# Two squares summed on TensorE, and a rule by which the planner lets an engine wait

## The chip, the cores and the metric

The kernel runs on one core of a Trainium2 chip. A core has TensorE (PE, matmuls into PSUM), VectorE (DVE), ScalarE (ACT), GpSimd (POOL) and SyncE (SP), which issues most of the DMAs. The metric is the time of one execution on the device in microseconds (us), taken as the median of several runs. The profile is of one more execution; its rows give times from the start of its span.

## What is computed

Two layers work on 512 latent tokens of width 1024 with a prefix of 256 context tokens. Each layer normalises and modulates the tokens, makes one wide projection, runs three kinds of attention over groups of its columns, gates the result and projects it back:

```python
def layer(x, cx, ...):
    mod = c_silu @ ada_w + ada_b                      # mod_c likewise, for the context
    shift, scale, gate = split(mod, 3)
    hx = rmsnorm(x, norm_w) * (1 + scale) + shift     # hc likewise
    px, pc = split_cols(hx @ w_in), split_cols(hc @ w_in)
    ya = global_gqa(...)            # all latent and context keys, rotary, normalised q and k
    yb = neighbourhood_attn(...)    # a clamped 2-D window, learned bias
    yc = window_gqa(...)            # +-128 tokens, a sink logit
    ux = concat(ya, yb, yc) * silu(px[9])
    x = x + gate * (ux @ w_out)
```

`rmsnorm(x, w)` is `x * rsqrt(mean(x*x) + 1e-6) * w`. After the second layer the latent tokens are normalised once more and returned. The context is carried only as far as the second layer needs it.

## The kernel before

**Tiling.** Activations are held transposed: width on the 128 partitions, in 8 blocks (`KT = 8`), tokens along the free dimension. The latent set is 128x512 a block, the context set 128x256. All products are fp32 made of two parts: a tensor is split into a rounded high part and a low part (names ending in h and l: `wh`/`wl`, `hL` for latent and `hC` for context activations), and PE adds three matmuls for each product. `split` does that for weights: `ws` arrives by DMA, ACT rounds it to `wh` (L245), DVE or POOL subtracts for `wl` (L248). In the attention, `pth` and `ptl` are the two parts of a transposed P, `P` the weights of the softmax; P goes to memory and comes back gathered as `R` (tiles R5 and R2), which PE transposes (L1049). `negm` (L1218) is the row maximum that the next stage waits for, and `OT` (L1069) gathers the attention's output from the bank `Obig`.

**The first norm.** `load_x(0)` issues eight DMAs for the latent blocks, `load_x(1)` eight for the context. `norm_x(s)` calls `add_sq` for each of the eight blocks of set `s`: ACT squares the block (L342), DVE adds the square to the first one (L346), and at the eighth PE multiplies the sum with a column of ones (L350), once for each 128 tokens (four times for the latent set, twice for the context), into the bank `Obig`. `rstd_rows` scales that (L357), POOL raises it to the power -1/2 (L359), PE spreads the result over the partitions (L367), and ACT copies it as `rb` (L390). `make_h` multiplies each block by it and by the modulation (L397) and splits it into `hL` or `hC` (L398, L400), with which the first projections start (L419). Beside it runs the modulation: `ada` multiplies silu(c) with weights that stream in (L213), ACT copies (L217, `adasb`), PE transposes (L221) and DVE finishes (L224 to L230, into tiles `mod`).

**The change of layers.** While the last attention of a layer runs, `reload` brings its gated results back (`uf`) and splits them (L481) into `qt`, `kt`, `hL`, `hC` and others; these are names of buffers that are used again, and here they hold the input of the output projection. `head` begins the output projection of the first blocks (`out_mm`, L508) in the `pj` and `Sbig` banks, and `block` finishes each: it loads the old stream `xr` by DMA (L551), DVE adds it times the gate to the bank (L561, `xn`), and `add_sq` starts the next norm's sum. DVE also computes part of the second layer's modulation itself, as dot products (L154): the gate from tiles `dots` of 128x512 (their DMAs L171 and L175, `junk512` their unused elementwise result), and the shift from rows: `row` (L682) holds silu(c) spread over the partitions and `dw` (L689) the weights, two dots of 128x1024 for each of eight `dw`. The tiles `row`, `dw` and `kept` (output weights that stay, split at L248 too) share one set of buffers in a pool that opens when buffers of the layer before are released, among them `hC` (L481) and `u` (L1377, L1379).

**What sets the order.** No order is written by hand. `arrange` takes all instructions as `Step`s with a modelled cost (`busy`, and for DMAs `move`), builds their dependences in a `Graph`, and calls `run(rank)`: a list schedule over five engines, in modelled time. Each engine takes, of the instructions that are ready by now (`now[e]`), the one of the best rank; those that get ready later are in `later[e]`. A rank is minus the time that still lies behind the instruction on its longest path, in ns, so a smaller rank is more urgent. `back` finds these times from a finished schedule, and the loop goes six turns, each with the ranks of the turn before. The schedule with the earliest modelled end gives each engine's stream, which is then fixed by added dependences:

```python
    for _ in range(CFG["turns"]):
        start, end, busy, streams = graph.run(rank)
        if best is None or max(end) < best[0]:
            best = max(end), streams
        at = graph.back(start, end, busy)
        rank = [(-t, k) for k, t in enumerate(at)]
```

So on the chip each engine works through a fixed list and waits, in order, for the next instruction's inputs.

Of the kernel before, what the change touches and what calls it, by code (L numbers as in the profile page):

```python
# [21 lines left out]
KT = 8  # L22
# [43 lines left out]
def body(tc, xT, small, bcast, rpb, adaw, adat, wt, wf, wo, trigA, trigQ, trigC, mskB, mskC, outT):  # L66
    nc = tc.nc
# [16 lines left out]
    ones = const.tile([128, 2], F32)  # L84
# [26 lines left out]
    Obig = ps.tile([128, 512], F32)  # L111
# [158 lines left out]
    def en(kind):  # L270

        turn[kind] = turn.get(kind, -1) + 1
        return nc.vector if EN[kind][turn[kind] % len(EN[kind])] == "D" else nc.gpsimd
# [62 lines left out]
            with tc.high_priority(offset=CFG["hp"]):  # L336
                done(p[:, 0:512].rearrange("p (t c) -> p t c", t=2), t2)

    def add_sq(sums, x, kt, n, pool, bank=psO):

        sq = pool.tile([128, NT], F32, name="sq", bufs=3)
        nc.scalar.activation(sq[:, 0:n], x, AF.Square)  # L342
        if kt == 0:
            sums.append(sq)
            return
        en("sq").tensor_add(sums[0][:, 0:n], sums[0][:, 0:n], sq[:, 0:n])  # L346
        if kt == KT - 1:
            pss = bank()
            for t in range(n // 128):
                nc.tensor.matmul(pss[:, 2 * t:2 * t + 2], sums[0][:, t * 128:(t + 1) * 128], ones,  # L350
                                 start=(t == 0), stop=True, skip_group_check=True)
            sums.append(pss)

    def rstd_rows(pss, n, pool, out):
        k = n // 128
# [17 lines left out]
    with tc.tile_pool(name="p0", bufs=1, reuse_waits="tile") as p0:  # L373
        xs = {}
# [9 lines left out]
        def norm_x(s):  # L384
            n = SETS[s][1] - SETS[s][0]
            sums = []
            for kt in range(KT):
                add_sq(sums, xs[s, kt], kt, n, p0, lambda: Obig[:, s * 8:])
            r = p0.tile([128, n], F32, name=f"rb{s}")
            nc.scalar.activation(r, rstd_rows(sums[1], n, p0, Sbig[:, s * 512:s * 512 + n])[:, 0:n], AF.Copy)  # L390
            rb[s] = r
# [137 lines left out]
    for l in range(2):  # L529
# [3 lines left out]
        with tc.tile_pool(name=f"p2_{l}", bufs=1, reuse_waits="tile") as p2:  # L533
# [139 lines left out]
            xs, sums = ({}, {}), ([], [])  # L673
# [67 lines left out]
            n = 0  # L741
# [853 lines left out]
BANKS = ("pj", "T", "Sbig", "Obig")  # L1595
TO_PE, TO_OTHER, TO_LAND = 400.0, 150.0, 700.0
SLOW = 21000.0
ISSUE = dict(tB=580.0, R5=520.0, R2=520.0, wr=680.0)
WAIT = {"PE": 53.0, "POOL": 78.0, "ACT": 36.0, "DVE": 36.0, "SP": 30.0}
BEHIND = {"ACT": 112.0, "DVE": 85.0, "POOL": 45.0}  # L1600
# [93 lines left out]
class Graph:  # L1694
# [76 lines left out]
    def run(self, rank):  # L1771

        steps, n = self.steps, len(self.steps)
        left = [len(b) for b in self.before]
        ready = [0.0] * n
        start, end, spent = [0.0] * n, [0.0] * n, [0.0] * n
        later = {e: [] for e in ENGINES.values()}
# [25 lines left out]
        while done < n:  # L1803
# [13 lines left out]
                    heapq.heappush(now[e], ((-1e18, 0), min(same)[1]))  # L1817
            r, k = heapq.heappop(now[e])
            s = steps[k]
            need, wait = t, None  # L1820
            for name in self.opens[k]:
                tag = self.tag[name]
# [246 lines left out]
```

## Time and profile before

| | us |
|---|---|
| median of 3 runs | 1146.3 |
| lowest, highest | 1142.51, 1149.14 |
| the profiled execution, device time | 1148.5 |
| its span | 1146.7 |
| PE busy (7352 records) | 1106.9 (97%) |
| DVE busy | 778.3 (68%) |
| ACT busy | 675.8 (59%) |
| POOL busy | 401.1 (35%) |

The span runs from the first to the last instruction; the device time of the same execution is 1.8 us longer. A row of the timeline gives start and length in us, engine, line, operation, output <- inputs (buffer numbers left out), the shapes, how many records are taken together, and in brackets the idle time ahead with what ended it. A matmul of fp32 that is not split shows as two records. `SPq` is the sequencer of SP while it issues DMAs. A row of a list of waits gives the waiting instruction, what released it, and the total, the number and the longest of these waits. Matmuls overlap their successors, so a record's length is more than its distance to the next.

### The profile page before, as it was taken

To read this page: it belongs to the slowest core of one execution; us is meant where nothing else is said; L and a number is where in the kernel's file an instruction comes from. 1 tells how busy PE (TensorE), PEld (TensorE's weight loads), DVE (VectorE), ACT (ScalarE), POOL (GpSimd) and SP (SyncE) were. 2 spreads that over 40 slices of the span, in tenths; PEclk is the share of its full clock that TensorE was granted. 3 is DMA by queue.
4 is the path that set the end of the run, shared out by engine and by line. 5 is a ranking of instruction groups with operands and counts; after the bars stand their busy time and mean duration, and the time that the engine had idled before them with its cause. 6 is when DMAs were issued, how large, how long until landed. Compare 5 with 4: busy or idle time off the path is not lost.

```text
span 1146.7 us, 21341 instructions
## 1 busy us (share of the span) xinstructions
PE 1106.9 (97%) x7352; PEld 974.5 (85%) x7352; DVE 778.3 (68%) x1642; ACT 675.8 (59%) x1454; POOL 401.1 (35%) x352
## 2 busy tenths in 40 slices
PE   5999999999999999999899999999999999999996
PEld 3799989998888888888687989998988888888886
DVE  5767667656657777668879764778565567677753
ACT  5546556465656667768623643555556677778651
POOL 1542102145452364526400021221156656556001
PEclk8999999999999999999999999999999999999998
DMA  9455446445464555456768543555344554557452
GB/s 356 180 154 191 140 135 193 137 152 165 157 204 151 191 174 185 160 186 217 252 227 267 166 148 98 169 182 152 126 144 157 161 180 163 194 177 228 140 175 74
DMA packets 111541, 200.96 MB, mean 175 GB/s; under 512 B 13676, under 2 KB 32456, under 8 KB 111432
## 3 DMA queue, kind: packets, MB, share of 16 engines
q1 hardware_dynamic: 103440, 184.01, 49.3%
q10 hardware_dynamic: 7992, 15.58, 4.1%
q8 instruction: 58, 0.95, 0.4%
q14 instruction: 51, 0.42, 0.1%
HBM read 116.46 MB, written 11.25 MB: 111 GB/s over the span
## 4 chain that ended last, share of the span: by engine, by line
PE 79%; DMA 6%; DVE 5%; ACT 3%; issue 3%; POOL 3%; SPq 1%; ACTq 0%; DVEq 0%; POOLq 0%
PE pj L311 29%; PE Obig L1033 9%; PE Sbig L1033 9%; PE T L1049 6%; PE pj L332 6%; PE pj L508 5%; DMA R<-P 4%; PE T L508 4%; PE Sbig L508 2%; PE Sbig L419 2%; PE T L311 2%; PE pj L419 1%; DVE junk L154 1%; PE Sbig L332 1%; DMA dw<-adat_dram 1%
## 5 line engine op out<-in xcount | busy, mean ns | idle before, releaser
L311 PE MATMUL pj<-hL,wh 128*128 128x512 f32 x880 | 293.1, 399 | 0.7 <-ACT tR L995 0.5
L1029 DVE TENSOR_TENSOR ptl<-T,pth 128x512 fp32r<-128x512 f32 (+1 forms) x264 | 172.5, 670 | 70.4 <-ACT pth L781 68.2
L781 ACT ACTIVATE pth<-T 128x512 fp32r<-128x512 f32 (+1 forms) x264 | 147.3, 580 | 73.3 <-PE T L1049 64.4
L311 PEld LDWEIGHTS pj<-hL,wh 128*128 128x128 f32 x880 | 158.8, 188 | 27.3 <-issue 1.7
L311 PE MATMUL pj<-hL,wl 128*128 128x512 f32 x440 | 174.8, 397 | 0.0
L245 ACT ACTIVATE wh<-ws 128x512 fp32r<-128x512 f32 x192 | 119.9, 629 | 93.1 <-PE pj L311 37.4
L1033 PE MATMUL Sbig<-kt,qt 128*128 128x256 f32 (+1 forms) x864 | 159.4, 305 | 0.9 <-DVE negm L1218 0.8
L248 POOL TENSOR_TENSOR wl<-ws,wh 128x512 fp32r<-128x512 f32 x76 | 100.2, 1320 | 145.1 <-ACT wh L245 126.0
L1033 PEld LDWEIGHTS Sbig<-kt,qt 128*128 128x128 f32 x864 | 127.6, 189 | 11.2 <-DVE negm L1218 1.8
L1049 PEld LDWEIGHTS T<-identr,R 128*128 128x128 f32 x1024 | 106.8, 140 | 27.4 <-DMA R<-P 7.4
L1033 PE MATMUL Obig<-pth,vt 128*128 128x256 f32 (+2 forms) x432 | 125.9, 307 | 2.2 <-DVE OT L1069 1.5
L1033 PE MATMUL Obig<-ptl,vt 128*128 128x256 f32 (+2 forms) x432 | 123.8, 306 | 0.2
L1049 PE MATMUL T<-identr,R 128*128 128x128 f32 x1024 | 114.5, 242 | 8.4 <-DMA R<-P 7.2
L248 DVE TENSOR_TENSOR wl<-ws,wh 128x512 fp32r<-128x512 f32 x116 | 84.9, 738 | 40.2 <-ACT wh L245 30.0
L311 PE MATMUL pj<-hC,wh 128*128 128x256 f32 x512 | 98.8, 284 | 0.0
L311 PEld LDWEIGHTS pj<-hL,wl 128*128 128x128 f32 x440 | 82.7, 188 | 15.0 <-issue 0.9
L1033 PEld LDWEIGHTS Obig<-pth,vt 128*128 128x128 f32 x432 | 81.3, 188 | 10.1 <-DVE OT L1069 2.1
L1033 PEld LDWEIGHTS Obig<-ptl,vt 128*128 128x128 f32 x432 | 81.2, 188 | 6.1 <-DVE negm L1117 0.5
L311 PEld LDWEIGHTS pj<-hC,wh 128*128 128x128 f32 x512 | 82.1, 190 | 2.1 <-DVE rs L881 0.2
L1115 DVE CUSTOM_DVE_ANT_0 P<-Sbig,rs 128x768 f32<-128x768 f32 (+1 forms) x80 | 65.7, 845 | 25.5 <-PE Sbig L1033 17.9
L1118 ACT ACTIVATE P<-P,negm 128x768 f32<-128x768 f32 (+1 forms) x80 | 67.5, 846 | 22.5 <-DVE negm L1117 16.7
L1459 POOL TENSOR_TENSOR bm<-wr,bm 128x192 f32<-128x192 f32 (+1 forms) x48 | 41.6, 893 | 97.3 <-DMA bm<-mskB_dram 64.6
(340 smaller groups left out, 2288.4 us busy)
## 6 DMA issues: line engine op xcount, KB each, us to landing
R<-P SPq DMA_DIRECT2D x216, 256.0 KB
ws<-wf_dram SPq DMA_DIRECT2D x120, 256.0 KB
ada<-adaw_dram SPq DMA_DIRECT2D x32, 512.0 KB
ws<-wo_dram SPq DMA_DIRECT2D x57, 256.0 KB
bm<-mskB_dram SPq DMA_DIRECT2D x16, 576.0 KB
R<-P SPq DMA_DIRECT2D x64, 128.0 KB
ws<-wt_dram SPq DMA_DIRECT2D x24, 256.0 KB
tB<-tA SPq DMA_DIRECT2D x72, 64.0 KB
```

Of the source, the lines that this page charges most:

```text
L245: nc.scalar.activation(hi, src, AF.Copy)
L248: eng.tensor_sub(lo, src, hi.bitcast(F32))
L311: nc.tensor.matmul(p[:, 0:n], a[:, r, :], cols(b[kt], c0, n), start=(i == 0), stop=(i == 23))
L332: nc.tensor.matmul(p[:, t * 256:(t + 1) * 256], tok(a[kt], t2 + t), b[:, r, :], start=(i == 0), stop=(i == 23))
L508: nc.tensor.matmul(p[:, 0:n], a[:, r, :], ucols(ua[b][ft], c0, n), start=(ft == FT_ORDER[0] and i == 0), stop=(ft == FT_ORDER[-1] and i == 2))
L781: nc.scalar.activation(out, src, AF.Copy)
L1029: nc.vector.tensor_sub(lo[:, 0:n], T[:, 0:n], hi[:, 0:n].bitcast(F32))
L1033: return nc.tensor.matmul(*args, **kw)
L1049: return nc.tensor.transpose(out.bitcast(F32R), src, identr)
L1115: nc.vector.tensor_tensor_reduce(out=P, in0=S, in1=r.to_broadcast([128, n]), op0=OP.mult, op1=OP.max, scale=1.0, scalar=-3.0e38, accum_out=m)
L1118: nc.scalar.activation(P, P, AF.Exp, bias=nm, accum_out=unit.stat("sums", i))
L1459: nc.gpsimd.tensor_add(b, src, b)
```

## The change

It has two parts. In `add_sq`, the squares of the last two latent blocks of the first norm (`alone`, blocks 6 and 7) are no longer added on DVE. PE multiplies the sum of blocks 0 to 5 with the ones (four matmuls), then the square of block 6 (four), then that of block 7 (four), all accumulating in the bank: twelve matmuls in place of four, and five adds in place of seven. Added dependences (`after`) keep them behind the first of them. The context set and all other norms take the old path.

In `run`, an engine other than PE looks ahead before it takes an instruction. If one that is more urgent by over 3000 ns (`HOLD`) gets ready before the one at hand would be done (`long`, for a DMA the longer of issue and transfer), the engine takes only an instruction that ends by then (60 ns of grace) or else stays idle until then. The rule acts in the model, when the order is made; on the chip only the order differs.

```diff
--- before.py
+++ after.py
@@ -336,20 +336,29 @@
             with tc.high_priority(offset=CFG["hp"]):
                 done(p[:, 0:512].rearrange("p (t c) -> p t c", t=2), t2)
 
-    def add_sq(sums, x, kt, n, pool, bank=psO):
+    sums_first = []
+
+    def add_sq(sums, x, kt, n, pool, bank=psO, alone=()):
 
         sq = pool.tile([128, NT], F32, name="sq", bufs=3)
         nc.scalar.activation(sq[:, 0:n], x, AF.Square)
         if kt == 0:
             sums.append(sq)
             return
-        en("sq").tensor_add(sums[0][:, 0:n], sums[0][:, 0:n], sq[:, 0:n])
-        if kt == KT - 1:
-            pss = bank()
+        if kt not in alone:
+            en("sq").tensor_add(sums[0][:, 0:n], sums[0][:, 0:n], sq[:, 0:n])
+        if kt == KT - 1 - len(alone):
+            sums.append(bank())
+            sq = sums[0]
+        if len(sums) == 2:
             for t in range(n // 128):
-                nc.tensor.matmul(pss[:, 2 * t:2 * t + 2], sums[0][:, t * 128:(t + 1) * 128], ones,
-                                 start=(t == 0), stop=True, skip_group_check=True)
-            sums.append(pss)
+                m = nc.tensor.matmul(sums[1][:, 2 * t:2 * t + 2], sq[:, t * 128:(t + 1) * 128], ones,
+                                     start=(len(sums) == 2 and t == 0 and kt == KT - 1 - len(alone)), stop=kt == KT - 1,
+                                     skip_group_check=True)
+                if alone and (t or kt > KT - 1 - len(alone)):
+                    after(m, sums_first[0])
+                elif alone:
+                    sums_first[:] = [m.ins.name]
 
     def rstd_rows(pss, n, pool, out):
         k = n // 128
@@ -385,7 +394,7 @@
             n = SETS[s][1] - SETS[s][0]
             sums = []
             for kt in range(KT):
-                add_sq(sums, xs[s, kt], kt, n, p0, lambda: Obig[:, s * 8:])
+                add_sq(sums, xs[s, kt], kt, n, p0, lambda: Obig[:, s * 8:], () if s else (KT - 2, KT - 1))
             r = p0.tile([128, n], F32, name=f"rb{s}")
             nc.scalar.activation(r, rstd_rows(sums[1], n, p0, Sbig[:, s * 512:s * 512 + n])[:, 0:n], AF.Copy)
             rb[s] = r
@@ -1595,6 +1604,7 @@
 BANKS = ("pj", "T", "Sbig", "Obig")
 TO_PE, TO_OTHER, TO_LAND = 400.0, 150.0, 700.0
 SLOW = 21000.0
+HOLD = dict(DVE=3000.0, ACT=3000.0, POOL=3000.0, SP=3000.0)
 ISSUE = dict(tB=580.0, R5=520.0, R2=520.0, wr=680.0)
 WAIT = {"PE": 53.0, "POOL": 78.0, "ACT": 36.0, "DVE": 36.0, "SP": 30.0}
 BEHIND = {"ACT": 112.0, "DVE": 85.0, "POOL": 45.0}
@@ -1817,6 +1827,20 @@
                     heapq.heappush(now[e], ((-1e18, 0), min(same)[1]))
             r, k = heapq.heappop(now[e])
             s = steps[k]
+            if e in HOLD:
+                long = max(s.busy, s.move) if s.dma else s.busy
+                soon = [x for x, y, _ in later[e] if y[0] < r[0] - HOLD[e] and x < t + long]
+                if soon:
+                    x = min(soon)
+                    fit = [z for z in now[e] if t + steps[z[1]].busy <= x + 60]
+                    heapq.heappush(now[e], (r, k))
+                    if not fit:
+                        free[e] = x
+                        continue
+                    r, k = min(fit)
+                    now[e].remove((r, k))
+                    heapq.heapify(now[e])
+                    s = steps[k]
             need, wait = t, None
             for name in self.opens[k]:
                 tag = self.tag[name]
```

Lines from 346 on stand 3 to 9 lines later in the changed kernel, and those behind `HOLD` 10 and more; L508 there is L517, L154 and L213 keep their numbers. Buffers from the first norm on have numbers 6 higher (`pj_6946` becomes `pj_6952`).

**The start, on PE.** The first rows of PE's stream before; `sq_151` is the sum of the squares, `ada` weights of the modulation, `T` a bank, `pj_219` the bank of the first projection:

```order
L350 MATMUL Obig_94<-ones_83,sq_151 128x2 x4
L213 MATMUL T_247<-ada_131,silu_c_95 2x256 x4
L213 MATMUL T_247<-ada_133,silu_c_95 2x256 x4
L367 MATMUL Sbig_93<-ident_72,rstd_179 128x128 x4
L221 MATMUL T_247<-ident_72,adasb_257 128x128 x2
L213 MATMUL T_312<-ada_221,silu_c_95 2x256 x4
L142 MATMUL T_369<-ident_72,silu_c_95 128x128 x4
L213 MATMUL T_312<-ada_223,silu_c_95 2x256 x4
L221 MATMUL T_312<-ident_72,adasb_322 128x128 x2
L350 MATMUL Obig_94<-ones_83,sq_187 128x2 x2
L419 MATMUL pj_219<-hL_243,wh_227 128x512
```

The same in the changed kernel (`sq_172` and `sq_178` are the squares of blocks 6 and 7):

```order
L355 MATMUL Obig_94<-ones_83,sq_151 128x2 x4
L355 MATMUL Obig_94<-ones_83,sq_172 128x2 x4
L355 MATMUL Obig_94<-ones_83,sq_178 128x2 x4
L213 MATMUL T_253<-ada_131,silu_c_95 2x256 x4
L213 MATMUL T_253<-ada_133,silu_c_95 2x256 x4
L376 MATMUL Sbig_93<-ident_72,rstd_185 128x128 x4
L221 MATMUL T_253<-ident_72,adasb_263 128x128 x2
L213 MATMUL T_318<-ada_227,silu_c_95 2x256 x4
L213 MATMUL T_318<-ada_229,silu_c_95 2x256 x4
L142 MATMUL T_375<-ident_72,silu_c_95 128x128 x4
L221 MATMUL T_318<-ident_72,adasb_328 128x128 x2
L142 MATMUL T_454<-ident_72,silu_c_95 128x128 x4
```

The two new groups stand behind the sum, ahead of the modulation's matmuls; behind them the two groups on `ada_227` and `ada_229` now stand together, and a second L142 group has come ahead of the context's sums and the first projection, which follow behind these rows.

**Near the end of the first layer's attention, on PE.** Before, two first matmuls that need `kt_6919` stand ahead of transposes of `R` (`T_7236<-identr` is the last of them); behind these come the other four on it, and only then those of another output block, in `Sbig`:

```order
L1049 MATMUL T_7236<-identr_77,R5_7183 128x128
L1049 MATMUL T_7236<-identr_77,R5_7206 128x128
L508 MATMUL pj_6946<-kt_6919,wh_6942 128x512
L508 MATMUL pj_6946<-kt_6919,wl_6943 128x512
L508 MATMUL pj_7129<-kt_6919,wh_7125 128x512
L508 MATMUL pj_7129<-kt_6919,wl_7126 128x512
L508 MATMUL Sbig_93<-hL_6849,wh_7352 128x512
L508 MATMUL Sbig_93<-hL_6851,wh_7352 128x512
L508 MATMUL pj_6946<-kt_6924,wh_6936 128x512
L508 MATMUL pj_7129<-kt_6924,wh_7119 128x512
```

In the changed kernel, where `kt_6925` is the same buffer and `wh_7358` the same weight as `wh_7352`:

```order
L517 MATMUL pj_6952<-kt_6925,wh_6948 128x512
L517 MATMUL pj_7135<-kt_6925,wh_7131 128x512
L517 MATMUL Sbig_93<-hL_6855,wh_7358 128x512
L517 MATMUL Sbig_93<-hL_6857,wh_7358 128x512
L517 MATMUL Sbig_93<-hL_6855,wl_7359 128x512
L517 MATMUL Sbig_93<-hL_6865,wh_7358 128x512
L517 MATMUL Sbig_93<-hL_6867,wh_7358 128x512
L517 MATMUL Sbig_93<-hL_6865,wl_7359 128x512
L517 MATMUL Sbig_93<-hL_6875,wh_7358 128x512
L517 MATMUL Sbig_93<-hL_6877,wh_7358 128x512
L517 MATMUL pj_6952<-kt_6925,wh_6948 128x512
L517 MATMUL pj_6952<-kt_6925,wl_6949 128x512
```

The first two on `kt` now stand behind the transposes, and eight matmuls of the `Sbig` block between them and the next on it.

**The change of layers, on DVE.** Before, around the last gate dots (`junk512`; behind each a row reads its accumulator, left out here), `hL` and `hC`:

```order
L154 ISA junk512_8680,mod1_2_105<-dots_8345,mod1_2_105 128x512
L1069 TENSOR_TENSOR OT_7135<-Obig_94,OT_7135 64x256
L154 ISA junk512_8709,mod1_2_105<-dots_8346,dots_8345,mod1_2_105 128x512
L481 TENSOR_TENSOR hL_7329<-u_7313,hL_7327 128x512
L1374 SCALAR_TENSOR_TENSOR OT_7135<-OT_7135,T_7322 128x256
L154 ISA junk512_8729,mod1_2_105<-dots_8346,dots_8345,mod1_2_105 128x512
L1379 TENSOR_TENSOR u_7313<-OT_7135,gc_6606 128x256
L154 ISA junk512_8752,mod1_2_105<-dots_8346,dots_8345,mod1_2_105 128x512
L248 TENSOR_TENSOR wl_7383<-ws_7380,wh_7382 128x512
L248 TENSOR_TENSOR wl_7389<-ws_7386,wh_7388 128x512
L481 TENSOR_TENSOR hC_7330<-u_7313,hC_7328 128x256
```

After (`OT_7141` is the `OT_7135` of before, `dots_8351` the `dots_8345`; the dot `junk512_8502` is `junk512_8496` there):

```order
L154 ISA junk512_8502,mod1_2_105<-dots_8352,dots_8351,sm_79 128x512
L1078 TENSOR_TENSOR OT_7141<-Obig_94,OT_7141 64x256
L490 TENSOR_TENSOR hL_7335<-u_7319,hL_7333 128x512
L1383 SCALAR_TENSOR_TENSOR OT_7141<-OT_7141,T_7328 128x256
L1388 TENSOR_TENSOR u_7319<-OT_7141,gc_6612 128x256
L490 TENSOR_TENSOR hC_7336<-u_7319,hC_7334 128x256
L248 TENSOR_TENSOR wl_7389<-ws_7386,wh_7388 128x512
L248 TENSOR_TENSOR wl_7395<-ws_7392,wh_7394 128x512
L154 ISA junk512_8554,mod1_2_105<-dots_8351,mod1_2_105 128x512
L248 TENSOR_TENSOR wl_7401<-ws_7398,wh_7400 128x512
L154 ISA junk512_8610,mod1_2_105<-dots_8352,dots_8351,mod1_2_105 128x512
```

`hL` and `hC` now stand ahead of the dots 8554 to 8662 (8548 to 8656 before), and the last four dots of before (8680 to 8752) have gone behind the dots on `dw`.

**The change of layers, on SP.** Before, the issues around `row` and the first `dw`:

```order
L171 DMA dots_8345<-adat_dram 128x512
L171 DMA dots_8346<-adat_dram 128x512 x3
L500 DMA ws_7506<-wo_dram 128x512
L500 DMA ws_7512<-wo_dram 128x512
L551 DMA xr_7339<-xT_dram 128x512
L551 DMA xr_7368<-xT_dram 128x512
L682 DMA row_7398<-spread_106 128x1024
L682 DMA row_7400<-spread_106 128x1024
L689 DMA dw_7402<-adat_dram 128x1024
L689 DMA dw_7404<-adat_dram 128x1024
L689 DMA dw_7455<-adat_dram 128x1024
L500 DMA ws_7518<-wo_dram 128x512
```

After:

```order
L171 DMA dots_8352<-adat_dram 128x512
L175 DMA dots_8351<-spread_106 128x512
L171 DMA dots_8352<-adat_dram 128x512
L691 DMA row_7404<-spread_106 128x1024
L691 DMA row_7406<-spread_106 128x1024
L698 DMA dw_7408<-adat_dram 128x1024
L698 DMA dw_7410<-adat_dram 128x1024
L509 DMA ws_7512<-wo_dram 128x512
L698 DMA dw_7461<-adat_dram 128x1024
L509 DMA ws_7518<-wo_dram 128x512
L560 DMA xr_7345<-xT_dram 128x512
L560 DMA xr_7374<-xT_dram 128x512
```

The rows and two `dw` now come ahead of the weights `ws_7512` and `ws_7518` (`ws_7506` and `ws_7512` before) and of both `xr`; four loads of `dots` are gone from ahead of them.

## The prediction

> **What bounds the kernel.** I read the busy shares first, then the span cut into stages, then what TensorE waited for. The page begins:
>
> ```profile
> span 1146.7 us, 21341 instructions
> PE 1106.9 (97%) x7352; PEld 974.5 (85%) x7352; DVE 778.3 (68%) x1642; ACT 675.8 (59%) x1454; POOL 401.1 (35%) x352
> ```
>
> PE is busy for 97% of the span, and the change takes no long matmul away. So what can be won is PE's idle time, 39.8 us. The busy time by stage says where it lies; each row gives the stretch, its length, then busy time and count of PE, PEld, DVE, ACT and POOL, the granted clock, the DMA share and GB/s:
>
> ```profile
> 0.00:30.00 30.00, 17.06 (x108) 10.39 (x109) 16.86 (x53) 16.32 (x35) 6.65 (x11) 0.89 0.97 358
> 30.00:510.00 480.00, 477.33 (x3409) 425.13 (x3408) 326.67 (x721) 292.51 (x653) 183.21 (x160) 1.00 0.52 167
> 510.00:540.00 30.00, 28.18 (x199) 25.02 (x198) 24.80 (x56) 25.73 (x58) 19.89 (x14) 1.00 0.66 202
> 540.00:565.00 25.00, 21.08 (x115) 16.29 (x114) 22.65 (x43) 17.91 (x43) 14.39 (x10) 0.95 0.84 277
> 565.00:615.00 50.00, 47.95 (x258) 40.75 (x256) 38.62 (x76) 13.61 (x24) 0.00 (x0) 0.99 0.73 253
> 615.00:1130.00 515.00, 507.85 (x3218) 450.24 (x3219) 343.92 (x688) 308.18 (x638) 172.07 (x152) 1.00 0.50 160
> ```
>
> Idle is length less PE's busy time: 12.9 us in the start, 6.0 around the change of layers (540 to 615), 1.8 before it, 2.7 and 7.2 in the two long stages, and what is left in the tail, whose order the change leaves alone. The waits of PE (total, times, longest) name the rest:
>
> ```profile
> PE Obig L350 <- DVE sq L346: 10.7, 1, 10.7
> PE T L1049 <- DMA R<-P: 7.2, 9, 1.9
> PE T L841 <- DVE qd L837: 0.6, 1, 0.6
> ```
>
> The first belongs to the start. The second, 7.2 us, is most of the idle time in the long stages (9.9 together): P goes to memory and comes back as R, and only an earlier P would help.
>
> **Part one, squares of the first norm.** These rows of the timelines (start, length) carry it: PE's sums, the same sums in the second layer, the context's sums, and three stretches of DVE.
>
> ```profile
> 10.71 1.87 PE L350 MATMUL Obig<-ones,sq 128*128 128x2 f32 x8 [10.71 <-DVE sq L346]
> 640.01 0.95 PE L350 MATMUL Obig<-ones,sq 128*128 128x2 f32 x8
> 20.58 0.85 PE L350 MATMUL Obig<-ones,sq 128*128 128x2 f32 x4
> 7.54 2.28 DVE L346 TENSOR_TENSOR sq<-sq 128x512 f32<-128x512 f32 x3 [0.15 <-ACT sq L342]
> 15.18 1.48 DVE L346 TENSOR_TENSOR sq<-sq 128x256 f32<-128x256 f32 x3 [1.42 <-ACT sq L342]
> 16.57 0.23 DVE L224 TENSOR_REDUCE mod<-T 128x2 f32<-128x8 f32 x2
> 15.23 0.63 PE L221 MATMUL T<-ident,adasb 128*128 128x128 f32 x2
> ```
>
> Four matmuls show as eight records, so twelve are 24. Of the seven adds the fifth becomes the last; it is the second of the three from 7.54, done at 7.54 + 2/3 of 2.28 = 9.1. PE begins there, 1.6 us sooner. Four records took 0.85 at 20.58, 0.21 each, so 24 take 5.1 and the sums end at 14.2, not 12.6: +1.6. At the pace of 640.01 (0.95 for 8) they take 2.9 and end at 12.0: -0.6. The first row has the slow pace, and the same kind of start is ahead of it, so I take the slow pace for most: +1.3. The two adds that go save nothing beyond that; they were the wait.
>
> The order also takes three context adds (1.48) from ahead of the modulation's reduce. That reduce began at 16.57 although its input was done at 15.23 + 0.63 = 15.9, so 0.7 comes back. The first normalised block is then 0.6 late. Most of this is covered: the DMA row of the start shows a share of 0.97 at 358 GB/s, so the weights and not the block set when PE runs dense. I take **+0.3**, bounds -1.0 (the pace of 640.01, and the adds) and +1.6 (all of it reaches the end).
>
> The clock could decide that pace. Two stretches of 3.4 us, each with the one behind it:
>
> ```profile
> 16.44:19.85 3.41, 1.42 (x16) 0.52 (x12) 2.84 (x10) 2.25 (x7) 0.00 (x0) 1.00 1.03 375
> 19.85:26.68 6.83, 6.58 (x28) 4.30 (x29) 3.81 (x12) 3.10 (x7) 1.46 (x2) 0.50 1.03 413
> 559.10:562.50 3.40, 1.44 (x13) 1.24 (x12) 3.29 (x8) 1.84 (x6) 3.40 (x2) 1.00 0.59 213
> 562.57:565.98 3.41, 3.32 (x8) 2.65 (x9) 3.41 (x9) 1.38 (x4) 0.03 (x1) 0.50 0.74 229
> ```
>
> PE was 42% busy in the first and third, and granted half the clock right after. So a stretch that PE no longer idles through saves 1.7 us behind it (half of 3.41). [...]
>
> **Part two, the waiting rule.** It lets DVE, ACT, POOL and SP leave work that is not urgent and wait. It adds no instruction; it moves some. Where it matters is the change of layers, 540 to 620. PE's waits there:
>
> ```profile
> PE Sbig L508 <- DVE kept L248: 1.8, 1, 1.8
> PE pj L508 <- POOL kt L481: 1.4, 1, 1.4
> PE Sbig L1033 <- DVE negm L1218: 0.8, 1, 0.8
> PE Obig L1033 <- DVE OT L1069: 0.7, 1, 0.7
> PE pj L508 <- ACT hL L480: 0.5, 1, 0.5
> PE pj L508 <- POOL hL L481: 0.4, 1, 0.4
> PE pj L508 <- DVE hL L481: 0.3, 1, 0.3
> ```
>
> They add up to 5.9. The rows behind them:
>
> ```profile
> 552.25 0.75 DVE L154 CUSTOM_DVE_ANT_0 junk<-dots,sm 128x512 bf16<-128x512 f32 x1
> 556.24 1.77 DVE L154 CUSTOM_DVE_ANT_0 junk<-dots,sm 128x512 bf16<-128x512 f32 x1
> 586.45 0.41 DVE L481 TENSOR_TENSOR hC<-u,hC 128x256 fp32r<-128x256 f32 x1
> 586.94 0.90 SPq L551 DMA_DIRECT2D xr<-xT_dram  x2
> 587.88 1.24 SPq L682 DMA_DIRECT2D row<-spread  x2
> 589.22 8.86 DMA dw<-adat_dram
> 585.25 1.29 DVE L248 TENSOR_TENSOR wl<-ws,wh 128x512 fp32r<-128x512 f32 x2
> 590.00:598.00 8.00, 8.00 (x43) 6.83 (x42) 2.71 (x4) 1.27 (x2) 0.00 (x0) 1.00 0.94 346
> 598.23 1.28 DVE L154 CUSTOM_DVE_ANT_0 junk<-dw,row,sm 128x1024 bf16<-128x1024 f32 x1 [3.73 <-DMA dw<-adat_dram]
> 591.10 0.75 DVE L561 SCALAR_TENSOR_TENSOR xn<-pj,mod,xr 128x512 f32<-128x512 f32 x1 [1.13 <-DMA xr<-xT_dram]
> 596.64 0.40 PE L508 MATMUL pj<-hC,wh 128*128 128x256 f32 x2
> ```
>
> - negm and OT. A gate dot (L154) stands just ahead of each on DVE. The first (0.75) moves 23 places back, the second (1.77) ten. The wait of 0.8 loses the first dot's length, 0.7, and the wait of 0.7 is shorter than the second dot: -1.4. Nothing that is wanted soon stands behind the dots themselves.
> - kt. PE stood 1.4 us for POOL's split. Eight Sbig matmuls whose operands are long ready move ahead; eight such records took 3.32 at half the clock (562.57), so 1.7 at the full clock that 559.10 shows. POOL is not faster, PE has other work: -1.4. Also the stretch 559.10 to 562.50 fills from 1.44 to over 2.8, so the 1.7 us of half clock behind it may go. Nothing says how full is enough, so I take 1.0 of 1.7.
> - hL. The last dots move behind hL and hC, so DVE's wait of 0.3 goes. Those on ACT and POOL (0.9) have no moved work ahead; they stay.
> - kept. This weight is the last of a long line: the buffers of row and dw come free with hC (586.45), the rows are issued from 587.88, the first dw lands at 589.22 + 8.86 = 598.1, and DVE then works through two dots of 1.28 for each of eight dw; kept stands among them. Now three dots of 0.75 (2.2) and the two wl of 585.25 (1.3) leave the way of hC, and two ws and two xr (0.93 + 0.90) that of the rows on SP: the rows are issued 5.3 sooner, at 582.6. Two rows and a dw (128x1024 f32, 0.52 MB each) take 6.2 at 253 GB/s (565 to 615) and about 2 for issue and landing, so dw is there near 591, 7 sooner. That is more than the wait, and the rest of it can't be won, since PE waits for nothing else of this line: -1.8.
> - xr, the price of it. The two xr now stand behind two rows, three dw and two ws, with their own 3.4 MB: 9.8 us at the 346 GB/s of 590 to 598, 13.4 at 253. From 582.6, with 2 for issue and landing, the first lands between 594.4 and 598, near 596 and not by 591.10. DVE also has four dw dots (5.1, from 591) ahead of that xn. PE needs the bank that it frees at 596.64; 596 and 0.75 for xn, with the next start, make it about 0.4 late, and half of the spread of the landing adds as much: **+0.9**, bounds 0 and +4.5 (landing at 598, one dot of 1.28 and the half clock that such a gap brings).
>
> Sum here: -1.4 - 1.4 - 1.0 - 0.3 - 1.8 + 0.9 = **-5.0**. Bounds: -7.6 (all 5.9 and 1.7, xr in time) and 0.
>
> **Elsewhere** several hundred instructions of DVE, ACT and SP move by one to three places. PE's waits in the long stages that aren't on R are 9.9 - 7.2 = 2.7, with 1.8 before the boundary: at most -4.5. For qd (0.6, above) and others of its kind the work ahead is now behind: I take -1.5. In return something newly late appears wherever a waited-for instruction is put behind another, such as a row scale of the first layer that now follows two modulation steps on DVE. I count three of the size of the negm wait (0.8): +2.4, bounds 0 and six, +4.8. Nothing for R: its chain keeps its P.
>
> **Sum**: +0.3 - 5.0 - 1.5 + 2.4 = -3.8. The profiled execution took 1148.5 by its own time (span 1146.7 and 1.8 around it), so 1144.7. It was 2.2 above the median of the runs, 1146.3, which gives 1142.5.
>
> **Rivals.**
> 1. *The gains come whole and little new is late.* The kept wait speaks for it: dw is so much sooner that DVE's dense stretch moves by several us. Boundary -7.0, elsewhere -3.0, start 0, new waits +0.5: -9.5, 1137. Against it: PE in the long stages has only 2.7 us to give. Chance 0.22.
> 2. *xr becomes the bound: slower.* Place: the bank needed at 596.64. If row and dw are not freed sooner (hC stays at 586.45, because it waits for u and not for the dots), the rows start at 586.9 and xr has 9.8 us of transfers and 2 of issue and landing behind that: it lands at 598.7. PE then stands 2.8 us with xn, and a dw dot of 1.28 can be in DVE's way, 4.1 together; a stretch that idle brings 1.7 of half clock; the kept wait stays. Boundary: -5.0 - 0.9 + 1.8 + 5.8 = +1.7. With start and the rest (+0.3 and +0.9) +2.9, or 1149; with the upper bounds of start and new waits +6.6, 1153. It decides from xr landing after 596. Chance 0.13.
> 3. *The gains are swallowed.* PE takes a bank or a weight a few hundred ns sooner and waits for the next one, and the new waits reach +4.8 or the half clock stays: -1.0, 1145. For it: R and DMA bounds remain, and only PE's idle can shrink. Chance 0.20.
>
> The forecast itself, -7 to -1, has 0.45.
>
> **Numbers.** Predicted 1142.5. Rival 1 reaches down to 1133 when boundary (-7.6), elsewhere (-4.5) and start (-1.0) all come at their lower bounds, -13.1; rival 2 reaches up to 1153. Of that upper part 2 us are left out, with less than 0.1 behind them: 1133 to 1151. A measurement of this kernel can tell about 0.5% (5.7 us) from no change. Faster by more: 0.20 of rival 1 and 0.16 of the forecast, 0.36. Slower by more: 0.07 of rival 2 and 0.04 of new waits beyond their bound, 0.11. Within: 0.53.
>
> **What would show it.** The sums of the first norm run from about 9.1 to between 13 and 14.4, and PE gets dense near 29 as before. The first dw dot starts by 594 and the wait for kept is gone; the waits for negm and OT are gone, and half clock at 562 with them. If the first xn stands late on xr and PE waits near 596, it is rival 2. If those waits go and the span does not fall by 4, look for new DVE waits in the long stages. Wrong would be a start later by over 2 us, or a span that moves in the long stages by more than 5.

## The result and the profile after

| kernel | median us | runs | ratio to before, 95% interval |
|---|---|---|---|
| before | 1145.85 | 6 | |
| changed | 1137.1 (1135.14 to 1138.49) | 6 | 0.9925 [0.9905, 0.9945] |

The change is 8.75 us, 0.75%, faster. The profiled execution after took 1136.6, near its kernel's median; that of before (1148.5) was 2.7 above its kernel's. So the two profiles differ by 11.9 us, three more than the kernels do. One execution of turns7 below was slow, 1196.44 us at a granted clock of 0.85; it stands in that kernel's median and not in its ratio.

First the page of the changed kernel, then the busy time by stage (columns as before; the work of a stage begins some us earlier after the change, so 1130 us cuts another piece off the end and that row is left out):

```profile
span 1134.8 us, 21310 instructions
PE 1103.8 (97%) x7368; PEld 975.7 (86%) x7368; DVE 760.9 (67%) x1640; ACT 674.9 (59%) x1454; POOL 399.9 (35%) x352
0.00:30.00 30.00, 18.10 (x101) 11.75 (x102) 13.05 (x44) 16.03 (x33) 6.02 (x10) 0.89 0.94 337
30.00:510.00 480.00, 477.15 (x3424) 426.03 (x3423) 317.09 (x724) 290.41 (x652) 184.79 (x160) 1.00 0.52 168
510.00:540.00 30.00, 29.57 (x212) 26.61 (x211) 27.68 (x64) 28.60 (x67) 19.77 (x14) 1.00 0.62 203
540.00:565.00 25.00, 22.45 (x125) 17.81 (x124) 21.99 (x41) 16.70 (x38) 13.84 (x9) 1.00 0.81 267
565.00:615.00 50.00, 48.64 (x265) 41.70 (x264) 44.27 (x81) 15.10 (x27) 0.00 (x0) 1.00 0.82 287
```

PE's idle time fell from 39.8 to 31.0 us. Between 540 and 565 PE is busy for 22.45 us where it was 21.08, and the granted clock is 1.00, not 0.95. The waits of PE over the whole span show the rest:

```profile
PE Obig L355 <- DVE sq L349: 10.0, 1, 10.0
PE T L1058 <- DMA R<-P: 2.5, 4, 0.8
PE T L142 <- ACT spr L145: 1.9, 1, 1.9
...
PE Obig L1042 <- DVE OT L1078: 1.5, 1, 1.5
PE pj L517 <- DVE xn L570: 1.4, 1, 1.4
PE T L1058 <- DVE ptl L1038: 1.2, 2, 0.8
PE T L1058 <- DVE negm L1126: 0.9, 2, 0.7
```

The waits for kept, for POOL's kt and for hL are gone. The wait for R has shrunk from 7.2 to 2.5, which the prediction did not give; a second profile of the kernel before has 5.1 of it, and one of the squares without the rule 3.2 (both below), so not all of that is the rule's. New is the wait for xn, 1.4.

### The profile page after: what moved, and what is told of

Same layout as the page of the kernel before. It is cut to its first block, busy times and chain, and to the rows that moved or that the text cites. A ratio compares the mean times of both kernels' runs of the same rounds, so it can differ in the third digit from the quotient of the medians.

```text
span 1134.8 us, 21310 instructions
## 1 busy us (share of the span) xinstructions
PE 1103.8 (97%) x7368; PEld 975.7 (86%) x7368; DVE 760.9 (67%) x1640; ACT 674.9 (59%) x1454; POOL 399.9 (35%) x352
```

## The experiments

Ratios are to runs of the kernel before on the same chip, whose median lay between 1144.35 and 1145.89; the groups of runs are from different chips. A ratio is an estimate of its own and need not be the quotient of two medians (for turns7 that quotient is 0.998). "Rule" is the waiting rule, "squares" the twelve matmuls.

| kernel | median us | ratio, 95% interval |
|---|---|---|
| rule_only | 1138.88 | 0.9944 [0.9928, 0.9960] |
| squares_only | 1145.33 | 0.9992 [0.9975, 1.0009] |
| warm_both | 1135.86 | 0.9918 [0.9901, 0.9936] |
| warm_rule_only | 1135.22 | 0.9913 [0.9892, 0.9934] |
| rule_sp | 1150.78 | 1.0053 [1.0028, 1.0078] |
| rule_no_sp | 1141.31 | 0.9978 [0.9966, 0.9991] |
| turns7 | 1142.29 | 0.9988 [0.9977, 1.0000] |
| before_again | 1145.57 (one run) | |
| splice_first | 1142.9 | 0.9969 [0.9950, 0.9988] |
| splice_mid | 1141.14 | 0.9957 [0.9939, 0.9975] |
| splice_last | 1139.25 | 0.9945 [0.9925, 0.9964] |
| r_first | 1144.4 | 0.9992 [0.9980, 1.0003] |

### The two parts apart

rule_only adds all squares on DVE again; squares_only empties the rule:

```diff
-add_sq(sums, xs[s, kt], kt, n, p0, lambda: Obig[:, s * 8:], () if s else (KT - 2, KT - 1))
+add_sq(sums, xs[s, kt], kt, n, p0, lambda: Obig[:, s * 8:], ())
```

```diff
-HOLD = dict(DVE=3000.0, ACT=3000.0, POOL=3000.0, SP=3000.0)
+HOLD = {}
```

> The waiting rule as in the change, all squares of the first norm added on DVE as before. In the profile of the changed kernel TensorE's work of the first 80 us stands 2.7 us later than before, and all that is won (some 14 us) comes behind that. Theory A, the squares on TensorE cost the start and the rule alone wins: the first norm's sums end near 12.6 again and the median is 2 to 3 us below that of the changed kernel, 1134 to 1135 (0.990 of before). Rival B, the late start of that profile came from transfers that landed late in that one execution, and the squares cost nothing: 1137 as with both parts (0.9925).

> The squares of blocks 6 and 7 on TensorE, the order made without the waiting rule. Theory A: slower than before by 1.5 to 2.7 us, 1147.5 to 1148.5 (1.0015 to 1.0025), with the sums of the first norm ending near 14.3 and the waits for R, kt and kept as before. Rival B: the same as before within 0.5 us. Rival C, the squares are what wins: 1137 to 1140.

The rule alone gives 0.9944 and the squares alone 0.9992, an interval that holds no change. So the rule wins and theory A falls: without the squares the kernel is not 2 to 3 us faster, its median is even 1.8 higher, in intervals that overlap. Rival C falls too. Rival B, that the squares cost nothing, is what squares_only shows. The timeline of PE in squares_only, its first rows:

```profile
9.40 5.28 PE L355 MATMUL Obig<-ones,sq 128*128 128x2 f32 x24 [9.40 <-DVE sq L349]
14.62 1.89 PE L213 MATMUL T<-ada,silu_c 128*2 128x256 f32 x16
...
22.07 0.78 PE L428 MATMUL pj<-hL,wh 128*128 128x512 f32 x1
```

The sums end near 14.6, 2.1 us later than before. If each of PE's instructions is matched with the same one of before, the median shift between 10 and 20 us is +2.1, and between 40 and 60 us +0.3. The loss is there and is made good in the 20 us behind it. In the changed kernel the shift stays between +2.6 and +2.9 up to 160 us, and in rule_only, whose squares are DVE's, it is +1.0: the late start of that profile is the rule's order and that execution together, not the squares alone.

### Is it the clock?

Both kernels got 24 matmuls ahead of everything on PE, whose result nothing reads:

```diff
+        for i in range(24):
+            nc.tensor.matmul(Obig[:, 384:512], ident, ident, start=True, stop=True, skip_group_check=True)
         norm_x(0)
         norm_x(1)
```

> The changed kernel with 24 matmuls of the identity with itself put ahead of everything on TensorE, into columns of the bank that nothing has read yet; they run while TensorE would wait for the first norm's squares. If the late start is the half clock's price on the 24 records of the sums (0.22 us each), these take 0.12 each and end near 12.5 instead of 15.2, and the time falls by 2 to 2.7 us to about 1134.7. If the start is set by the transfers, the sums end sooner and the time stays at 1137.

> The waiting rule with the squares added on DVE, and the same 24 matmuls ahead. Eight records of sums at the full clock save 0.9 us, and the modulation's matmuls behind them perhaps as much: 1 to 2 us below the rule alone, about 1133, if the half clock of the first 16 us is on the path; equal to the rule alone if transfers set the start.

PE's first rows in the changed kernel, then in warm_both:

```profile
9.97 5.28 PE L355 MATMUL Obig<-ones,sq 128*128 128x2 f32 x24 [9.97 <-DVE sq L349]
```

```profile
1.36 7.74 PE L419 MATMUL Obig<-ident 128*128 128x128 f32 x48 [1.36 <-POOL ident masks.py:199]
9.62 2.84 PE L355 MATMUL Obig<-ones,sq 128*128 128x2 f32 x24 [0.52 <-DVE sq L349]
13.21 2.17 PE L213 MATMUL T<-ada,silu_c 128*2 128x256 f32 x16 [0.75 <-DMA ada<-adaw_dram]
```

The 24 records took 2.84 us and not 5.28, 0.12 us each and not 0.22. So here what PE did in the 8 us ahead (matmuls for 7.74 of them) decides their pace. That the clock is behind it is not shown. The trace of the changed kernel holds no record of the granted clock before 19.44 us, and the windows read 1.00 over the slow sums (9.97 to 15.25); in squares_only they read 1.00 over the first 30 us, and its sums are as slow. The half clock of the expectations is the author's estimate. For it speaks that the four records at 20.58 before take as long, 0.21 each, where the granted clock is 0.50 (19.85 to 26.68).

The pace did not change within the sums: 5.28 for 24 records is the slow one to the end. Nor did it soon behind them: in squares_only PE is busy without a break from 9.40 to past 22.8, and eight records of L213 still take 1.03 us at 20.77, where they take 0.61 at 25.60. So the first 12 us in which this timeline shows PE busy throughout did not bring the fast pace.

Of the 2.4 us little reaches the end. The ada matmuls now wait 0.75 for their DMA, and the median is 1.2 lower in intervals that overlap widely. rule_only with the same matmuls is 3.7 lower (0.9913 against 0.9944), on four runs, with intervals that just overlap. Its profile doesn't show the gain at the start: the eight records of the sums take 1.05 us instead of 1.87, but they begin 0.7 later, the modulation's matmuls behind them run at the slow pace (1.03 for eight records, at 14.32), and between 40 and 120 us PE's work stands 1.2 later than in rule_only. What the slow pace at the start costs this kernel stays open.

### Which engine waits

`HOLD` was cut to SP alone, and to all but SP. turns7 has no rule and seven turns of the planner; before_again is the kernel before.

```diff
-HOLD = dict(DVE=3000.0, ACT=3000.0, POOL=3000.0, SP=3000.0)
+HOLD = dict(SP=3000.0)
```

```diff
-HOLD = dict(DVE=3000.0, ACT=3000.0, POOL=3000.0, SP=3000.0)
+HOLD = dict(DVE=3000.0, ACT=3000.0, POOL=3000.0)
```

```diff
-turns=6
+turns=7
```

> The waiting rule for SP alone, squares on DVE. Theory A, the queue of transfers is where the rule wins: loads that can wait no longer stand ahead of R, row and dw, the waits for R fall from 7.2 to 3, the first dw lands some 8 us sooner, and the time is near that of the rule on all four engines, 1138 to 1140 (0.994). Theory B, DVE's order wins (dots behind negm, OT, hL and hC): 1143 to 1146, with the waits for negm, OT, hL as before.

> The waiting rule for DVE, ACT and POOL, not SP. Theory A: near before, 1143 to 1146, with the waits for R as before. Theory B: 1138 to 1140, with the waits for negm, OT, hL and kt gone. Theory C, no engine in particular, the planner simply lands on another order each time: this, the run with SP alone and the run with a seventh turn all move by 2 to 7 us without any one wait in common.

> The kernel before with seven turns of the planner in place of six and nothing else: 460 of PE's instructions stand elsewhere. It measures what another order without the rule is worth. Theories A and B: within 3 us of before, 1143 to 1149. Theory C: it can win as much as the rule, 1137 to 1141.

> The kernel before once more, for a second profile of it: which of its waits are the order's and come again, and which are one execution's. If the waits for R of 1.4 us and more at 515, 940 and 1062 are the order's they are there again at the same places within 0.5 us each; if they are late transfers of that one execution, the total for R is 3 to 4 and not 7.2.

Theory A falls clearly: the rule on SP alone is slower, 1.0053. Without SP it wins 0.9978, less than half. Its interval and that of all four engines together do not overlap ([0.9966, 0.9991] and [0.9928, 0.9960]), so in these orders SP's part helps only with the others. Nor is it enough that R waits less: rule_sp has 4.8 us of waits for R in its profile where before had 7.2. Theory B holds in part: 1141.31 lies between the forecasts of A and B, and in the profile of rule_no_sp the waits for kt and OT in the change of layers are gone, while kept (0.9), hL (0.9) and negm (0.4) are still waited for. A seventh turn moves 460 of PE's instructions and brings 0.9988: another order by itself is worth about 1.4 us (2.1 by the medians), and rule_sp shows that it can be 6 the other way. Theory C is therefore not refuted as a part of the story: a share of the 8.75 us may be the luck of one order. The runs of rule_sp lie between 1145.65 and 1153.73, and its profile is of one at the lower end (1145.83), so where those at the upper end lose 5 us and more stays open.

The second profile of before answers what its waits are. The list of waits of PE in before_again, 30 to 1125 us:

```profile
PE T L1049 <- DMA R<-P: 5.1, 6, 1.4
PE Obig L1033 <- DVE OT L1069: 1.5, 2, 0.8
PE pj L508 <- POOL kt L481: 1.4, 1, 1.4
PE Sbig L508 <- DVE kept L248: 1.2, 1, 1.2
...
PE Sbig L1033 <- DVE negm L1218: 0.8, 1, 0.8
```

The larger waits come again at the same places. The three for R of 1.38, 1.41 and 1.86 are 1.11, 1.39 and 1.02 here, so the last differs by more than the 0.5 that was expected, and R's total of 5.1 lies between the two forecasts. That a larger wait is there belongs to the kernel and its order; its size varies by up to 0.9 us from one execution to the next.

### Stage by stage

To leave the planner's luck out, two finished orders of the same instructions were spliced: that of squares_only and that of the changed kernel. What the one plan starts before a cut comes first, and what is left follows in the order of the other (the lines ahead, left out here, make both plans, one with an empty `HOLD`):

```diff
+    done, mixed = set(), {e: [] for e in plans[0][1]}
+    for p, until in PARTS:
+        for e, ks in plans[p][1].items():
+            mixed[e] += [k for k in ks if k not in done and plans[p][2][k] < until]
+        done = {k for ks in mixed.values() for k in ks}
```

with `PARTS` (plan 1 has the rule) `((1, 478500), (0, 1e9))`, `((0, 478500), (1, 622000), (0, 1e9))` and `((0, 622000), (1, 1e9))`.

> The squares on TensorE, and two orders spliced: the rule's order (that of the changed kernel) for all that the planner starts in its first 478.5 us (500 us on the chip: the start and the first layer's attention but its end), and behind that the order made without the rule. By the shift of TensorE's work between the profiles of the two parents (the squares alone, 1145.3, and both parts, 1137.1) this stretch wins 1.8 of 8.8 us. Theory D, the gain is spread over stages and adds up: 1143.5. Theory E, it sits in the change of layers: 1145.3. Theory C, it is an order's luck that no stretch holds: no sum.

> The rule's order between 478.5 and 622 us of the planner's time (500 to 650 on the chip: the end of the first layer's attention and the change of layers), the order without it before and after. Theory D: 1 to 3 us, by the shift of the profiles 1.2, by the waits that go (kt 1.3, kept 1.3, negm 0.8, OT 0.7, hL 0.3, less xn 1.4) 3.0: 1142.3 to 1144. Theory E: all of it, 1137. If the prediction's -5.0 at this place was right: 1140.3.

> The rule's order from 622 us of the planner's time on (650 on the chip: the second layer), the order without it before. Theory D: 5.8 of the 8.8 us are here by the shift of the profiles, and the waits for R at 912, 938 and 1059 are gone: 1139.5. Theory E: 1145.3. The prediction gave the second layer nothing: +0.5.

Against squares_only (0.9992, on another chip) the rule's order wins 0.0023 in the first stretch, 0.0035 in the middle, 0.0047 in the last: 2.6, 4.0 and 5.4 us of 1145.8. The differences have half widths of some 3 us each, so the first is not clear of noise. Their sum, 12.0, is more than the 7.7 of the changed kernel over squares_only (0.9925), but within what these widths allow; all three lean on the one median of squares_only. Theory E falls: the order from 650 us on wins 5.4 by itself. Theory D stands, with shares that are rough. PE's waits by stretch, summed from the lists:

| us | 30 to 480 | 480 to 640 | 640 to 1125 | R in the last |
|---|---|---|---|---|
| before | 2.5 | 7.5 | 7.0 | 4.4 |
| before_again | 3.0 | 7.1 | 5.5 | 3.0 |
| squares_only | 3.0 | 5.8 | 5.6 | 1.5 |
| splice_first | 2.9 | 6.0 | 5.0 | 2.3 |
| splice_mid | 2.9 | 4.4 | 3.0 | 0.6 |
| splice_last | 2.3 | 6.5 | 2.1 | 0.6 |
| changed | 2.1 | 4.5 | 2.4 | 0.0 |

In the middle the rule's order has fewer waits: 4.4 and 4.5, against 5.8 to 6.5 in squares_only and the two splices without it there. In the first stretch there is no such difference (2.9 and 2.1 with it, 2.3 to 3.0 without). In the last, 2.1 and 2.4 with it stand against 5.6, 5.0 and 3.0 without; the 3.0 of splice_mid, whose order there is the old one, says how much one execution can differ: 2 to 3 us. R alone is 1.5, 2.3 and 0.6 there without the rule, 0.6 and 0.0 with it. The lists for 640 to 1125, splice_last first, then the changed kernel:

```profile
PE T L1058 <- DVE negm L1126: 0.7, 1, 0.7
PE Obig L1042 <- ACT pth L790: 0.6, 1, 0.6
PE T L1058 <- DMA R<-P: 0.6, 2, 0.3
PE T L1058 <- DVE ptl L1038: 0.2, 1, 0.2
```

```profile
PE T L1058 <- DVE negm L1126: 0.9, 2, 0.7
PE T L1058 <- DVE ptl L1038: 0.8, 1, 0.8
PE Obig L1042 <- ACT pth L790: 0.7, 1, 0.7
```

### Why R is no longer late

In SP's order the rule puts R ahead of loads of tB, ws and uf at three places where PE waited. r_first is the kernel before with only these rows of SP moved, eight of them (the expectation below says nine):

```diff
+    sp = best[1]["SP"]
+    outs = {k: {u[0].name for u in steps[k].use if u[1]} for k in sp}
+    for name, ahead_of in (("R2_6485", "R5_6484"), ("R2_11563", "tB_11585"), ("R5_11562", "R2_11563"), ("R5_11571", "tB_11585"),
+                           ("R2_13154", "ws_13670"), ("R5_13153", "R2_13154"), ("R2_13163", "ws_13670"),
+                           ("R5_13162", "ws_13670")):
+        at = [i for i, k in enumerate(sp) if name in outs[k]][-1]
+        to = [i for i, k in enumerate(sp[:at]) if ahead_of in outs[k]][-1]
+        sp.insert(to, sp.pop(at))
```

> The order of before on all engines, but nine rows of SP moved at three places, as the rule has them: R2_6485 ahead of R5_6484; R5_11562 and R2_11563 ahead of the third of four tB, R5_11571 ahead of the fourth; R5_13153, R2_13154, R2_13163 and R5_13162 ahead of ws_13670 and uf_13250. TensorE waited there 1.55, 1.58 and 2.00 in the first profile of before and 1.25, 1.54 and 1.15 in the second. Theory F, these waits are made by what stands ahead of R in SP's queue: they fall to 0.5 or less each and the time to 1142.0 to 1143.5 (0.997). Rival G, R waits for P or for the transfers in flight, whatever the queue's order: the three waits stay above 1 each and the time stays within 1 us of before. In both the place of the wait by 912, which the rule does not reorder, keeps its 0.7 to 0.9.

0.9992, no change that can be told: theory F falls, and the time is as rival G has it. At the first place the wait is 0.98 now, at the second 1.30 (as in the expectation, the distance to the matmul before less the usual distance of its kind). At the third R waits no longer, and PE waits 1.86 there for ptl instead, the next thing on its list:

```profile
1062.95 0.53 PE L1049 MATMUL T<-identr,R 128*128 128x128 f32 x4 [1.86 <-DVE ptl L1029]
```

The second place shows more when the DMA issues of ACT and SP are laid beside P's softmax on ACT (the timelines of ACT, SP and PE). Before:

```profile
932.50 0.94 ACT L1118 ACTIVATE P<-P,negm 128x768 f32<-128x768 f32 x1
933.47 1.16 ACTq L1361 DMA_DIRECT2D u<-r  x2
934.16 2.05 SPq L1044 DMA_DIRECT2D R<-P  x3
939.95 0.71 PE L1049 MATMUL T<-identr,R 128*128 128x128 f32 x4 [1.41 <-DMA R<-P]
```

In r_first:

```profile
933.01 0.93 ACT L1118 ACTIVATE P<-P,negm 128x768 f32<-128x768 f32 x1
933.95 1.24 ACTq L1361 DMA_DIRECT2D u<-r  x2
933.74 1.43 SPq L1044 DMA_DIRECT2D R<-P  x2
935.92 1.17 SPq L1044 DMA_DIRECT2D R<-P  x2
940.24 0.45 PE L1049 MATMUL T<-identr,R 128*128 128x128 f32 x3 [1.17 <-DMA R<-P]
```

In the changed kernel:

```profile
921.99 0.93 ACT L1127 ACTIVATE P<-P,negm 128x768 f32<-128x768 f32 x1
923.30 0.50 ACTq L1370 DMA_DIRECT2D u<-r  x1
922.63 2.04 SPq L1053 DMA_DIRECT2D R<-P  x2
925.67 1.18 SPq L1053 DMA_DIRECT2D R<-P  x2
```

Before, ACT's two transfers of u were issued from 0.7 us ahead of the first R on, and PE began the transposes 5.8 us after that R's issue. In the changed kernel one R is issued 0.7 us ahead of the first u and a second beside it, and PE, whose transposes stand there at 928.42 (5.8 after the issue), doesn't wait. r_first gets one R ahead, and the wait passes to a later one, issued at 935.92 behind u. One reading is that R is late because u, issued by ACT, is in flight ahead of it. It was not tried by itself (u moved alone), and squares_only, whose order has no rule, speaks against it. There, too, both u are issued ahead of the first R, and PE begins the transposes 3.8 us after that R's issue:

```profile
933.26 1.37 ACTq L1370 DMA_DIRECT2D u<-r  x2
935.10 1.82 SPq L1053 DMA_DIRECT2D R<-P  x3
938.86 0.69 PE L1058 MATMUL T<-identr,R 128*128 128x128 f32 x4 [0.51 <-DMA R<-P]
```

Another reading fits more of the traces. A transfer of R lands in 16 parts (all 312 of them in the profile of before). Of the R that ended the wait at 939.95 before, 15 parts had landed by 938.15 and the last at 939.81, and PE went on 0.14 us after that one. While it was under way the core's queues also moved one packet of 16 KB that the profile calls `instruction`, started at 937.59; in squares_only, while its first three R were under way, there was only one of 8 KB. These are the rows of the queues, before (934.78 to 939.81), then squares_only (935.10 to 938.73), with packets, MB and share:

```profile
q8 instruction: 1, 0.02, 1.2%
```

```profile
q14 instruction: 1, 0.01, 0.5%
```

At the other two places it is alike: 15 parts by 514.05 and 1059.46, the last at 515.09 and 1061.62, with a packet of 16 KB started at 509.84 and 1056.94; and before_again has such a packet ahead of all three waits (510.86, 935.81, 1056.00). Over all fourteen profiles, 747 transfers of R had a packet of 16 KB moving between their issue and the landing of the 15th part, and in 361 of them the last part came over 0.8 us behind the 15th; of the 3621 without one, in 51. So the late R goes with where these packets fall, and they fall elsewhere in another order or with other instructions: in squares_only the packet nearest to this place started at 932.98, ahead of R's issue. No run moved the packets alone, so the cause is not shown either; but as far as this is it, how long a plan waits for R is in part luck.

## Why the prediction held, and which step failed

**The likeliest time was 1142.5, the measured 1137.1**; it is inside the range of 1133 to 1151, but that is wide. The change of -8.75 lies outside the forecast's own -7 to -1 and is the first rival's size (1137), for which 0.22 was given; faster by more than 0.5% had 0.36. The range held, the sum did not give the size.

- **Start, +0.3: right for the squares.** DVE's add let PE begin at 9.4 in squares_only (9.1 forecast) and the 24 records took 5.28 (5.1 forecast). Most of the delay was covered, as forecast; squares_only measures -0.9 with a half width of 2. But in the profile of the changed kernel PE's work stands 2.6 to 2.9 us later up to 160 us, more than the 2 that the prediction had named as a sign of being wrong. As squares_only is back at +0.3 by 40 us, that is not the squares' doing; the rule's order at the start had no term in the sum.
- **Change of layers, -5.0: right in size.** splice_mid measures -4.0, with a half width of some 3. The waits for kt, kept and hL and the half clock behind kt are gone (granted 1.00 from 540 to 615, where before had 0.50 from 562.57 to 565.98); OT's wait of 0.7 has gone with its dot, and another for OT, 1.5, has come at 548. The term for the half clock, -1.0, hung on more than the wait for kt: squares_only, splice_first and splice_last wait 1.3 to 1.4 us for kt at the same place, and the granted clock is 1.00 there from 540 to 615. So that term isn't in splice_mid's -4.0. The step "xr, the price of it" had the place and nearly the size (1.4, forecast 0.9) but a cause that was half of it. These rows of the changed kernel's timelines show it:

```profile
582.88 0.92 SPq L560 DMA_DIRECT2D xr<-xT_dram  x2
586.82 1.28 DVE L154 CUSTOM_DVE_ANT_0 junk<-dw,row,sm 128x1024 bf16<-128x1024 f32 x1 [2.41 <-DMA dw<-adat_dram]
591.29 1.28 DVE L154 CUSTOM_DVE_ANT_0 junk<-dw,row,sm 128x1024 bf16<-128x1024 f32 x1
592.50 0.75 DVE L570 SCALAR_TENSOR_TENSOR xn<-pj,mod,xr 128x512 f32<-128x512 f32 x1
593.30 0.50 PE L517 MATMUL pj<-hC,wh 128*128 128x256 f32 x2 [1.36 <-DVE xn L570]
```

  xn started in the very moment when the fourth dw dot ended, with no wait for xr: the dots in DVE's queue were the price, not the transfer. dw came sooner than forecast (586.8 to 591). The 2 us that the forecast has for issue and landing are an estimate; a small transfer of before (r<-rT, at most 6 KB, issued at 830.35) took 2.52.
- **Elsewhere, -1.5 and +2.4, together +0.9: wrong.** This is the step that failed. splice_first and splice_last measure -2.6 and -5.4. The bound was too small by a misreading: of the 7.2 us of waits for R, 1.6 stand between 480 and 640 and not in the long stages, so these had 9.9 - 5.6 = 4.3 us of other idle time, not 2.7. And "Nothing for R: its chain keeps its P" was wrong: the prediction took R's waits, the largest that were left, as given by P because only an earlier P would help. The changed order has 2.5 of them. At the place looked at P came 10.5 us sooner, like its neighbours on PE, and the R that was waited for landed 12.1 sooner (927.73, the second R issued there, and 939.81 before). How much of R's part is the rule's stays open: squares_only, without the rule, has 3.2 and takes the time of before. Against squares_only, splice_last has 0.9 us less of R's waits in the last stretch and none of the 2.3 for qd, whose kind the prediction did count among those that go. Between the profiles of before and after PE's work comes a further 6.4 us sooner from 650 to 1125 us, more than the 5 that the prediction had named as a sign of being wrong; some of that is the 3 us by which the two profiles differ more than the kernels. The new waits in the last stretch (negm 0.9, ptl 0.8) are near what was counted, though fewer.
- **Rival 1** had the size, but with another sum: 7.0 at the change of layers and 3.0 elsewhere, where 4.0 and 8.0 were measured stage by stage, each within several us.

## What to carry to other kernels

A wait that recurs in a second profile of the same kernel is no accident of one execution; count it as a possible gain, not as nothing, even if the chain behind it looks fixed. Before it is put down to that chain, look at what else moved while it lasted: here the late R went with packets that the profile counts as `instruction`, apart from the transfers that the kernel issues (361 late of 747 with such a packet, 51 of 3621 without). To find where a planner's rule wins, splice two finished orders by stage: one rule for one engine alone gave another order everywhere, and one engine's order without the others' moved the wait to the next instruction.

## What was not expected

One engine's share of the rule was harmful alone: 1.0053 for SP, 0.9978 for the other three, 0.9944 for all. And 24 matmuls without use, in time that PE would have stood, made the next 24 records take 2.84 us in place of 5.28.
